# RMSNorm with repeated rows: squares of a tile in one ScalarE instruction, summed by VectorE

## The chip, the core and the metric

The kernel runs on one core of a Trainium2 chip. The core has a vector engine (VectorE, DVE in the profile), a scalar engine (ScalarE, ACT), a GpSimd engine (POOL), a matrix engine that this kernel does not use, and a sync engine (SP). SP and ACT each have a queue from which they start transfers (SPq and ACTq in the profile; the transfers of SP run on queue q1, those of ACT on q10). Sixteen DMA engines move the data between device memory (HBM) and the on-chip memory (SBUF, 128 partitions). The metric is the device time of one execution in microseconds; lower is better.

## The reference

The input `x` has the shape 8 x 512 x 2048 in float32, `gamma` has 2048 elements. Each row of `x` is written out twice in a row, normalized by its root mean square and multiplied by `gamma`:

```
x_rep = np.repeat(x, 2, axis=1)
rms = np.sqrt((x_rep ** 2).mean(axis=-1, keepdims=True) + 1e-6)
out = x_rep / rms * gamma
```

So 33.55 MB come in and 67.11 MB go out, and both copies of a row are the same.

## The kernel before, in words

The 4096 rows are cut into 8 tiles (`ntiles`) of 128 partitions by K = 4 rows. A tile `y` holds R x K = 8 rows per partition, called slots here: `load` (line 45) brings the four input rows into slots 4 to 7, and the result of row k is written to slot 2k and its copy to slot 2k + 1, so that the whole tile is one contiguous run of 64 KB per partition for the store. The writes run ahead of nothing that is still needed: row 0 is in slot 4, which is overwritten only by the result of row 2. The pool `rows` has three such tiles, so the load of tile i + 1 needs the buffer of tile i - 2 and waits for its store to land.

`square` (line 64) squares one row on ScalarE, writes the squares to a scratch tile `sq` in the matrix engine's accumulation memory (PSUM) where nobody reads them, and keeps the row's sum in `ss` by the instruction's accumulator output; it then takes the square root (line 71). `scale` (line 74) takes the reciprocal on VectorE and multiplies the row by it and by `gamma_b` in one instruction (line 77). `repeat` (line 82) copies the result into the neighbouring slot. `compute` (line 85) runs rows one by one: while VectorE scales row k, ScalarE squares row k + 1; the copies of rows 0 to 2 are made by ScalarE, the last one by VectorE.

The order of the work is written out by hand (`manual_schedule`): every engine does its instructions in the order in which the program names them. The loads of tiles 0, 1 and 2 stand at the start, on ACT's queue, the first in four parts. In the loop (line 107), the load of tile i + 1 is issued on ACT's queue ahead of the first square of tile i, from i = 2 on; the load of the last tile has two parts. `store` (line 55) issues on SP's queue once the last copy of its tile is done; the last tile is computed and stored in two halves. The store of tile 5 is cut into runs of 32 KB, all others of whole tiles into runs of 64 KB.

Of the kernel before, what the change touches and what calls it, by code (L numbers as in the profile page):

```python
# [1 line left out]

# [4 lines left out]


@with_exitstack
def kernel(  # L10
    ctx: ExitStack,
    tc: tile.TileContext,
    x: bass.AP,
    gamma: bass.AP,
    out: bass.AP,
):
    nc = tc.nc
    P = nc.NUM_PARTITIONS
    f32 = mybir.dt.float32
    Act = mybir.ActivationFunctionType  # L20
    Alu = mybir.AluOpType

    B, S, D = x.shape
    Bo, So, Do = out.shape
    R = So // S
    assert R == 2 and D == Do and B == Bo and So == S * R
    eps = 1e-6
    inv_d = 1.0 / float(D)


    K = 4
    N = B * S
    assert N % (P * K) == 0
    ntiles = N // (P * K)
    x_t = x.rearrange("b s d -> (b s) d").rearrange("(n p k) d -> n p k d", p=P, k=K)
    out_t = out.rearrange("b s d -> (b s) d").rearrange("(n p j) d -> n p (j d)", p=P, j=K * R)

    singles = ctx.enter_context(tc.tile_pool(name="singles", bufs=1))
    rows = ctx.enter_context(tc.tile_pool(name="rows", bufs=3))
    junk = ctx.enter_context(tc.tile_pool(name="junk", bufs=1, space=bass.MemoryType.PSUM))  # L40
    small = ctx.enter_context(tc.tile_pool(name="small", bufs=8))

    ys = []

    def load(i, eng, parts=1):


        y = rows.tile([P, K * R, D], f32, name="y")
        step = K // parts
        for k in range(0, K, step):  # L50
            at = K * (R - 1) + k
            eng.dma_start(out=y[:, at : at + step, :], in_=x_t[i, :, k : k + step, :])  # L52
        ys.append(y)

    def store(i, k0, k1):

        run = 32768 if i == ntiles - 3 else 65536
        nc.sync.dma_start(  # L58
            out=out_t[i, :, R * k0 * D : R * k1 * D],
            in_=ys[i][:, R * k0 : R * k1, :].rearrange("p j d -> p (j d)"),  # L60
            max_dma_last_dim=run,
        )

    def square(i, k):
        sq = junk.tile([P, D], f32, name="sq")
        ss = small.tile([P, 1], f32, name="ss")
        nc.scalar.activation(  # L67
            out=sq[:], in_=ys[i][:, K * (R - 1) + k, :], func=Act.Square, accum_out=ss[:]
        )
        rms = small.tile([P, 1], f32, name="rms")  # L70
        nc.scalar.activation(out=rms[:], in_=ss[:], func=Act.Sqrt, scale=inv_d, bias=eps_t[:])  # L71
        return rms

    def scale(i, k, rms):
        rstd = small.tile([P, 1], f32, name="rstd")
        nc.vector.reciprocal(out=rstd[:], in_=rms[:])  # L76
        nc.vector.scalar_tensor_tensor(  # L77
            out=ys[i][:, R * k, :], in0=ys[i][:, K * (R - 1) + k, :], scalar=rstd[:], in1=gamma_b[:],
            op0=Alu.mult, op1=Alu.mult,
        )  # L80

    def repeat(i, k, copy):
        copy(out=ys[i][:, R * k + 1, :], in_=ys[i][:, R * k, :])  # L83

    def compute(i, k0, k1):

        rms = square(i, k0)
        for k in range(k0, k1):
            scale(i, k, rms)
            if k + 1 < k1:  # L90
                rms = square(i, k + 1)
                repeat(i, k, nc.scalar.copy)
            else:
                repeat(i, k, nc.vector.tensor_copy)


    ctx.enter_context(tc.manual_schedule())
    load(0, nc.scalar, parts=K)
    gamma_b = singles.tile([P, D], f32, name="gamma_b")
    nc.sync.dma_start(out=gamma_b[0:1, :], in_=gamma.partition_broadcast(1))  # L100
    nc.gpsimd.partition_broadcast(out_ap=gamma_b[:], in_ap=gamma_b[0:1, :])  # L101
    eps_t = singles.tile([P, 1], f32, name="eps_t")
    nc.vector.memset(eps_t, eps)  # L103
    load(1, nc.scalar)
    load(2, nc.scalar)

    for i in range(ntiles):


        if i >= 2 and i + 1 < ntiles:  # L110
            load(i + 1, nc.scalar, parts=2 if i + 2 == ntiles else 1)
        parts = 2 if i == ntiles - 1 else 1
        for k in range(0, K, K // parts):
            compute(i, k, k + K // parts)
            store(i, k, k + K // parts)


# [1 line left out]
_INS = ['x', 'gamma']  # L119
_OUTS = [((8, 1024, 2048), 'float32')]  # L120


# [23 lines left out]
```

## Time and profile before

| | |
|---|---|
| median of 3 runs | 240.74 us (240.67 to 244.2) |
| the profiled execution | 240.8 us, of which the span is 239.0 us |
| moved | 100.69 MB, mean 421 GB/s over the span |
| VectorE busy | 90.8 us (38%), 74 instructions |
| ScalarE busy | 115.8 us (48%), 121 instructions |
| squares (line 67) | 32 of 1872 ns, each with an accumulator read of 186 ns |
| square roots (line 71) | 32 of 294 ns |
| reciprocals (line 76) | 32 of 162 ns |
| scales (line 77) | 32 of 2352 ns |
| copies on ScalarE, on VectorE (line 83) | 23 of 1888 ns, 9 of 1226 ns |

The page gives the busy time of each engine, then the span in 40 slices of 5.98 us with a digit for the busy share in each, then the DMA queues, the chain of work that ended last, and the groups of instructions by line. Times in the timeline are in us from the start of the span. Waits of an engine are listed with what ended them.

### The profile page before, as it was taken

Reading aid. Unit: us, or ns where it says so; the run is one execution under the profiler, and the core shown is the slowest. Engines: PE = TensorE matmul, PEld = TensorE weight load, DVE = VectorE, ACT = ScalarE, POOL = GpSimd, SP = SyncE. Lnnn points to the kernel's source line nnn. Section 1 sums busy time; section 2 is a strip of 40 time slices with the busy share of each in tenths; the row PEclk is TensorE's granted clock in tenths of the full one; section 3 lists DMA queues with packets and bytes.
Section 4 is the critical chain, followed back from the end, with each engine's and each line's share of the span. In section 5 each row is a group of like instructions: output and inputs, shape, how many; then the busy total and the mean of one; then the engine's idle time right before and its main releaser. Section 6 shows DMA issues by size and latency. Waiting matters only on the chain.

```text
span 239.0 us, 295 instructions
## 1 busy us (share of the span) xinstructions
DVE 90.8 (38%) x74; ACT 115.8 (48%) x121; POOL 2.5 (1%) x5
## 2 busy tenths in 40 slices
DVE  0477846006560047600666007460076490072000
ACT  3998992009940089500994019930499550180000
POOL 4000000000000000000000000000000000000000
DMA  7999989989979989999899899799999999898994
GB/s 267 428 447 439 439 351 439 526 351 439 515 345 455 450 374 494 395 411 510 362 428 526 351 439 528 345 444 433 400 430 444 406 499 436 384 505 356 439 428 192
DMA packets 3156, 100.69 MB, mean 421 GB/s; under 512 B 337, under 2 KB 337, under 8 KB 337
## 3 DMA queue, kind: packets, MB, share of 16 engines
q1 hardware_dynamic: 1426, 67.12, 65.0%
q10 hardware_dynamic: 1728, 33.56, 33.3%
q14 instruction: 2, 0.02, 0.0%
HBM read 33.56 MB, written 67.11 MB: 421 GB/s over the span
## 4 chain that ended last, share of the span: by engine, by line
DMA 71%; ACT 10%; DVE 8%; ACTq 1%; issue 0%; SPq 0%
DMA y<-in_x_dram 38%; DMA out_dram<-y 33%; DVE y L77 6%; ACT sq L67 6%; ACT y L83 3%; DVE y L83 2%; ACTq L52 1%; ACT rms L71 1%; DVE rstd L76 0%; SPq L58 0%
## 5 line engine op out<-in xcount | busy, mean ns | idle before, releaser
L67 ACT ACTIVATE sq<-y 128x2048 f32<-128x2048 f32 x32 | 59.9, 1872 | 90.3 <-DMA y<-in_x_dram 74.4
L77 DVE SCALAR_TENSOR_TENSOR y<-y,rstd,gamma_b 128x2048 f32<-128x2048 f32 x32 | 75.3, 2352 | 1.2
L76 DVE RECIPROCAL rstd<-rms 128x1 f32<-128x1 f32 x32 | 5.2, 162 | 123.6 <-ACT rms L71 123.6
L83 ACT COPY y<-y 128x2048 f32<-128x2048 f32 x23 | 43.4, 1888 | 3.6 <-DVE y L77 3.6
L83 DVE COPY y<-y 128x2048 f32<-128x2048 f32 x9 | 11.0, 1226 | 0.3
L71 ACT ACTIVATE rms<-ss,eps_t 128x1 f32<-128x1 f32 x32 | 9.4, 294 | 1.0
L67 ACT ACTIVATION_READ_ACCUMULATOR sq<-y 128x1 f32 x32 | 6.0, 186 | 0.0
L67 ACT ACT_TABLE_LOAD x1 | 1.3, 1283 | 4.1 <-issue 4.1
L101 POOL PARTITION_BROADCAST gamma_b<-gamma_b x1 | 2.3, 2295 | 2.4 <-DMA gamma_b<-in_gamma_dram 2.4
L71 ACT ACT_TABLE_LOAD x1 | 1.3, 1283 | 0.0
L103 DVE MEMSET eps_t<- 128x1 f32 x1 | 0.1, 59 | 0.8 <-PEq L130 0.8
L130 POOL MEMSET const-float32-0.0<- 128x1 f32 x1 | 0.1, 100 | 0.2 <-issue 0.2
L130 POOL MEMSET const-bfloat16-1.0<- 128x1 bf16 x1 | 0.1, 102 | 0.0
L130 POOL MEMSET const-uint8-127<- 128x1 uint8 x1 | 0.1, 102 | 0.0
L130 POOL MEMSET const-float32-1.0<- 128x1 f32 x1 | 0.1, 100 | 0.0
## 6 DMA issues: line engine op xcount, KB each, us to landing
y<-in_x_dram ACTq DMA_DIRECT2D x6, 4096.0 KB, 32.6
out_dram<-y SPq DMA_DIRECT2D x1, 8192.0 KB
out_dram<-y SPq DMA_DIRECT2D x2, 4096.0 KB, 26.4
y<-in_x_dram ACTq DMA_DIRECT2D x4, 1024.0 KB, 7.7
y<-in_x_dram ACTq DMA_DIRECT2D x2, 2048.0 KB, 29.9
out_dram<-y SPq DMA_DIRECT2D x6, 37.5
gamma_b<-in_gamma_dram SPq DMA_DIRECT2D x1, 8.0 KB
```

The costliest lines, as they stand in the source:

```text
L52: eng.dma_start(out=y[:, at : at + step, :], in_=x_t[i, :, k : k + step, :])
L67: nc.scalar.activation(out=sq[:], in_=ys[i][:, K * (R - 1) + k, :], func=Act.Square, accum_out=ss[:])
L71: nc.scalar.activation(out=rms[:], in_=ss[:], func=Act.Sqrt, scale=inv_d, bias=eps_t[:])
L76: nc.vector.reciprocal(out=rstd[:], in_=rms[:])
L77: nc.vector.scalar_tensor_tensor(out=ys[i][:, R * k, :], in0=ys[i][:, K * (R - 1) + k, :], scalar=rstd[:], in1=gamma_b[:], op0=Alu.mult, o ...
L83: copy(out=ys[i][:, R * k + 1, :], in_=ys[i][:, R * k, :])
L101: nc.gpsimd.partition_broadcast(out_ap=gamma_b[:], in_ap=gamma_b[0:1, :])
L103: nc.vector.memset(eps_t, eps)
L130: nc = _bacc.Bacc("TRN2", target_bir_lowering=False, num_devices=1)
```

## The change

Tiles 1 to 6 are computed in another way. One ScalarE instruction squares all four rows (8192 elements per partition) and writes the squares to slots 0 to 3 of the same tile, which hold nothing at that time; VectorE then sums them row by row with one `tensor_reduce` (`total`). Tile 1 does both in halves. One square root and one reciprocal serve the four rows; four scales follow; and the copies are two ScalarE instructions of two rows each. The load of tile i + 1 is issued on ACT's queue after the wide square of tile i, and is one transfer for the last tile too. Tile 0 and the first half of tile 7 keep the square with the accumulator output; in tile 0 the copies of the last two rows are one VectorE instruction. The second half of the last tile puts its squares into slots 1 and 3, which its first half has not filled yet.

At the start, the loads of tiles 0 (now in two parts), 1 and 2 move to SP's queue, and that of `gamma` to ACT's; ScalarE loads the function table that has the square root at once; and the constant `eps_t` is set by GpSimd. The stores all use runs of up to 64 KB. The pool `small` has 4 buffers of four columns.

```diff
-    small = ctx.enter_context(tc.tile_pool(name="small", bufs=8))
+    small = ctx.enter_context(tc.tile_pool(name="small", bufs=4))
...
     def store(i, k0, k1):
-
-        run = 32768 if i == ntiles - 3 else 65536
         nc.sync.dma_start(
             out=out_t[i, :, R * k0 * D : R * k1 * D],
             in_=ys[i][:, R * k0 : R * k1, :].rearrange("p j d -> p (j d)"),
-            max_dma_last_dim=run,
         )
...
+    def slots(i, k0, k1):
+        if i == ntiles - 1 and k0 == H:
+            return slice(1, R * H, R)
+        return slice(k0, k1)
+
+    def square_total(i, k, ss):
         sq = junk.tile([P, D], f32, name="sq")
-        ss = small.tile([P, 1], f32, name="ss")
         nc.scalar.activation(
-            out=sq[:], in_=ys[i][:, K * (R - 1) + k, :], func=Act.Square, accum_out=ss[:]
-        )
...
+            out=sq[:], in_=ys[i][:, K * (R - 1) + k, :], func=Act.Square, accum_out=ss[:, k : k + 1]
         )
...
+    def square(i, k0, k1):
+        nc.scalar.activation(
+            out=ys[i][:, slots(i, k0, k1), :], in_=ys[i][:, K * (R - 1) + k0 : K * (R - 1) + k1, :],
+            func=Act.Square,
+        )
...
+    def total(i, k0, k1, ss):
+        nc.vector.tensor_reduce(
+            out=ss[:, k0:k1], in_=ys[i][:, slots(i, k0, k1), :], op=Alu.add, axis=mybir.AxisListType.X
+        )
+
+    def rsqrt(k0, k1, ss, rstd):
+        nc.scalar.activation(
+            out=rstd[:, k0:k1], in_=ss[:, k0:k1], func=Act.Sqrt, scale=inv_d, bias=eps_t[:]
+        )
+        nc.vector.reciprocal(out=rstd[:, k0:k1], in_=rstd[:, k0:k1])
+
+    def scale(i, k0, k1, rstd):
         for k in range(k0, k1):
...
+            nc.vector.scalar_tensor_tensor(
+                out=ys[i][:, R * k, :], in0=ys[i][:, K * (R - 1) + k, :], scalar=rstd[:, k : k + 1],
+                in1=gamma_b[:], op0=Alu.mult, op1=Alu.mult,
+            )
+
+    def repeat(i, k0, k1, copy=nc.scalar.copy):
+        y_r = ys[i].rearrange("p (k r) d -> p k r d", r=R)
+        copy(out=y_r[:, k0:k1, 1, :], in_=y_r[:, k0:k1, 0, :])
...
-    load(0, nc.scalar, parts=K)
+    load(0, nc.sync, parts=2)
     gamma_b = singles.tile([P, D], f32, name="gamma_b")
-    nc.sync.dma_start(out=gamma_b[0:1, :], in_=gamma.partition_broadcast(1))
+    nc.scalar.dma_start(out=gamma_b[0:1, :], in_=gamma.partition_broadcast(1))
+    nc.scalar.preload_act_table(Act.Sqrt)
+    eps_t = singles.tile([P, 1], f32, name="eps_t")
+    nc.gpsimd.memset(eps_t, eps)
     nc.gpsimd.partition_broadcast(out_ap=gamma_b[:], in_ap=gamma_b[0:1, :])
-    eps_t = singles.tile([P, 1], f32, name="eps_t")
-    nc.vector.memset(eps_t, eps)
-    load(1, nc.scalar)
-    load(2, nc.scalar)
+    load(1, nc.sync)
+    load(2, nc.sync)
 
     for i in range(ntiles):
+        ss = small.tile([P, K], f32, name="ss")
+        rstd = small.tile([P, K], f32, name="rstd")
+        if i == 0:
+            for k0 in (0, H):
+                for k in range(k0, k0 + H):
+                    square_total(i, k, ss)
+                rsqrt(k0, k0 + H, ss, rstd)
+                scale(i, k0, k0 + H, rstd)
+            repeat(i, 0, H)
+            repeat(i, H, K, nc.vector.tensor_copy)
+        elif i < ntiles - 1:
+            for k0, k1 in ((0, H), (H, K)) if i == 1 else ((0, K),):
+                square(i, k0, k1)
+                total(i, k0, k1, ss)
...
-        if i >= 2 and i + 1 < ntiles:
-            load(i + 1, nc.scalar, parts=2 if i + 2 == ntiles else 1)
-        parts = 2 if i == ntiles - 1 else 1
-        for k in range(0, K, K // parts):
-            compute(i, k, k + K // parts)
-            store(i, k, k + K // parts)
+            if i >= 2:
+                load(i + 1, nc.scalar)
+            rsqrt(0, K, ss, rstd)
+            scale(i, 0, K, rstd)
+            repeat(i, 0, H)
+            repeat(i, H, K)
+        else:
+            for k in range(H):
+                square_total(i, k, ss)
+            rsqrt(0, H, ss, rstd)
+            square(i, H, K)
+            scale(i, 0, H, rstd)
+            total(i, H, K, ss)
+            rsqrt(H, K, ss, rstd)
+            repeat(i, 0, H)
+            store(i, 0, H)
+            scale(i, H, K, rstd)
+            repeat(i, H, K)
+        store(i, H if i == ntiles - 1 else 0, K)
```

Here H = K // 2 = 2.

## The prediction

> **What bounds the kernel now.** First the page's slices and the DMA queues. The DMA engines are busy in every slice but the first and the last, while VectorE and ScalarE work in bursts with pauses.
>
> ```profile
> DVE 90.8 (38%) x74; ACT 115.8 (48%) x121; POOL 2.5 (1%) x5
> DMA  7999989989979989999899899799999999898994
> DMA packets 3156, 100.69 MB, mean 421 GB/s; under 512 B 337, under 2 KB 337, under 8 KB 337
> ```
>
> Second, two stretches cut from one landing of a store to the next, with the columns stretch, length, busy time of DVE, ACT and POOL, PE clock, DMA share, GB/s:
>
> ```profile
> 80.60:109.60 29.00, 11.20 (x9) 14.36 (x15) 0.00 (x0) 1.00 1.00 434
> 109.65:138.64 28.99, 11.20 (x9) 14.36 (x15) 0.00 (x0) 1.00 1.00 434
> ```
>
> One tile (4.19 MB in, 8.39 MB out) takes W = 29.0 us of full DMA; at 434 GB/s a store alone is 19.3 us and a load 9.7. Third, the timeline of one tile (start, length, engine, line):
>
> ```profile
> 109.65 0.34 ACTq L52 DMA_DIRECT2D y<-in_x_dram  x1
> 113.31 1.88 ACT L67 ACTIVATE sq<-y 128x2048 f32<-128x2048 f32 x1 [14.14 <-DMA y<-in_x_dram]
> 129.02 1.23 DVE L83 COPY y<-y 128x2048 f32<-128x2048 f32 x1
> 130.33 0.33 SPq L58 DMA_DIRECT2D out_dram<-y  x1
> 138.64 0.33 ACTq L52 DMA_DIRECT2D y<-in_x_dram  x1
> ```
>
> From the first square to the store's issue it is 130.33 - 113.31 = 17.0 us: call this C. The load at 138.64 waits for a store to land, so the new store was queued 138.64 - 130.33 = 8.3 us before the ring was empty. That is the only slack. Compute is hidden as long as C grows by less than about 8 us. Fourth, who gets the DMA when a load and a store are both queued: in the window 85 to 108,
>
> ```profile
> q1 hardware_dynamic: 96, 6.29, 63.1%
> q10 hardware_dynamic: 111, 3.64, 36.6%
> ```
>
> (q1 is SP's queue, the stores; q10 ACT's, the loads). A load gets a little over a third: its rows are 32 KB long, the store's 64 KB. So a load issued beside a store is slow: 109.65 to about 142.3, 32.7 us, though alone it would take 9.7.
>
> **What the Trainium skill says.** "VectorE: DVE Perf Modes", The perf-mode tier table: tensor_reduce runs at 1x only, whatever the type. No reduce is in this trace; the 1x operation in it (L77, 2352 ns for 2048) is (2048 + 210)/0.96, as that rate wants. "ScalarE: Activation LUTs", What ACT_TABLE_LOAD costs: an ACTIVATE with immediate scale and bias takes 186 ns + 0.833 ns per element; for 2048 that is 1892, the trace has 1872 (L67) and 1888 (copy, L83), so it agrees. "DMA: Bandwidth & Descriptors", Queues, rings and completion order: an engine round-robins between the queues packet by packet; with 64 against 32 KB that is 2 to 1, and the 63 to 37 above agrees.
>
> **The new chain of one tile (tiles 2 to 6).** Wide square 8192 x 0.833 + 186 = 7.01 us (page's price; 4 x 1.87 = 7.5 from the row is the upper end). Reduce of 8192, which can't start earlier: (8192 + 151)/0.96 = 8.69 us, an estimate by the fit that the same VectorE page gives in its errata section for fp32 tensor_tensor; 8.75 by the 210 of L77. Sqrt 0.29, reciprocal 0.16. Four scales, back to back 2.38 each with the handoff (215.44 - 213.06 in the chain): 9.50. The last wide copy, 4096 x 0.833 + 186 = 3.60; the first lies beside scales 3 and 4. Six handoffs of 0.02 to 0.03: 0.15. Sum C' = **29.4 us**, 12.4 more than now. What was interleaved by row (square beside scale) is now serial. ACT is in order, so square(i+1) starts only after the last copy of tile i: C' is also the least period, against W = 29.0.
>
> Engine totals don't matter: ACT some 14.5 us and DVE 18.4 per tile.
>
> **The moved load.** load(i+1) now stands behind the wide square on ACT, 7.1 us after its start, no longer in front. It has store(i-2) to wait for, long landed by then; what is queued behind it (sqrt, copies) is idle anyway during the reduce. But until then the newest store has the DMA alone, and then has two thirds of it. The load ends last: with the store 7.1 us ahead, 12.2 us of it remain, over in 18.4; the load has had 6.1 of its 9.7 by then and 3.5 more alone. So it ends W after the store's first byte. Now add the latencies: issue to first byte 0.8 us and last byte to landing 1.8 us, estimates from the start (issue at 0.72, DMA share 0.56 already between 1 and 2 us; gamma lands at 2.79) and from the tail (last store lands 21.3 us after 216.77, at 238.1, when bytes had ended by about 236.3). If no load overlaps, square(i+1) comes 31.6 us after store(i-1)'s issue, and store(i) 29.4 after square(i): two tiles take 61.0 us where DMA alone would take 58.0.
>
> **The walk** (us). Start: loads 0 to 2 move from ACT's to SP's queue, gamma the other way. Tile 0 in two halves of 4.8 us each: the first lands at 0.72 + 2.1 (gamma's 0.72 to 2.79) + 4.8 = 7.6, the second at 12.5; two squares with their accumulator reads 4.1, to 16.6; sqrt and reciprocal 0.5, two scales 4.8, to 21.9; the DVE copy of both rows 2.3 to 2.5 (2 x 1.23): store 0 at 24.4, now 23.8. Covered: the DMA has load 2 until about 32, and store 0 is now behind it on the same ring. Were that cover gone it would cost 0.6. The table load saved (1.28), eps on POOL (0.1, before gamma lands) and four DMA issues of 0.3 to 0.9 on SP ahead of its first store lie in the same cover: nothing. Store 0 lands at 52.9 as now, bytes ended 51.1. Tile 1: square at 22.6, in halves 2 x 3.6, reduces of 4.42 end at 35.0, then 0.5, scales 45.1, copy: store 1 at 48.7, in time.
>
> - square 2 at 48.7, load 3 issued 55.8; store 1 + load 3 end 80.1, landing 81.9 = square 3. Store 2 at 78.1, in time.
> - store 2 + load 4 end 109.1. Store 3 at 81.9 + 29.4 = 111.3 = square 4, first byte 112.1: **DMA idle 3.0**.
> - store 3 + load 5 end 141.1, landing 142.9 = square 5. Store 4 at 140.7, first byte 141.5: idle 0.4.
> - store 4 + load 6 end 170.5. Store 5 at 172.3 = square 6, first byte 173.1: **idle 2.6**.
> - store 5 + load 7 end 202.1, landing 203.9 = square 7. Store 6 at 201.7: idle 0.4; its bytes end 221.9.
> - Last tile: squares, sqrt, scales and reduce 13.8, sqrt and reciprocal, first copy: half store at 203.9 + 17.8 = 221.7: idle 0.6. The second half follows at 226.6, behind 9.7 us of the first: in time.
>
> Idle in all 7.0 us, all on the path since the DMA has no slack. The removed 32 KB rows of the third-last store and the unsplit last load change no bytes; I take nothing, and from -1 to +1 us (one round of packets each way). The small pool's 4 buffers bring no wait: each is reused four tiles later.
>
> The profiled execution took 240.8 us with a span of 239.0; the median is 240.74, the same. **240.8 + 7.0 = 247.8, say 248**, 3% slower.
>
> **Bounds of the unknowns.** Latencies together between 2.1 (gamma) and 3.3: -1 to +2. Reduce and square together 1 us cheaper: less idle at two places, -2 or nothing, because a store issued sooner pushes its 64 KB rows (2.4 us) between the last rows of the load. Square at its upper end: +0.5 at three chains in a row, +1.5. This gives 245 to 252.
>
> **Rivals.**
> - *The cover holds* (ends on the other side, not slower). If a load got half of the DMA beside a store, it would land 19.4 + 2.6 = 22.0 us after issue, just inside the 22.3 that the chain still has; then stores come every 29.4 and the first backlog hides the 0.4: 241, at most 243. It decides from a share of one half up. The 63 to 37 and the landings of 32.7 us speak against it; that the split is by packet count (96 to 111) in a coarse window leaves it open. 0.15.
> - *The new forms cost more*: a reduce or a square into the tile's own slots that runs at, say, 3 us more per tile. C' of 32.4 then sets every period: about 6 x 3 less what overlaps, 253 to 260. L83's copy to the same memory at 1888 speaks against. 0.12.
> - *The DMA gets faster* from fewer mixed stretches: 434 GB/s is held in both mixed and pure stretches, so only the 1 to 2 us of dips could go; under 236 would need 2% more rate. 0.03.
>
> Forecast 0.68; 0.02 for a start that fails to hide. The range takes the forecast's 245 to 252, and reaches to 243 and to 254 into the two nearest rivals. Two per cent, 4.8 us, is about what a measurement of this kernel can tell from no change: slower by over 2% (above 245.6) is most of the forecast, the second rival and a little of the rest, 0.75; faster 0.03; within 0.22.
>
> **What would show it.** Square at 7.0 us, reduce 8.7, copy 3.6; square to store issue 29.4 in tiles 2 to 6; loads landing 24 to 26 us after issue; DMA share below 0.9 around 109 to 112 and 170 to 173, at 1.0 before 100; stores landing 30 to 31 us apart; ACT's waits for the load alternate between about 0 and 2 to 4 us. It is wrong if the load lands under 22 us from its issue (first rival), or if the DMA stays at 434 GB/s to the end.

## The result, and the profile after

The changed kernel takes 251.59 us (median of 4 executions, 249.72 to 253.26) against 240.70: 1.045 times the kernel before, 95% interval 1.034 to 1.055. The profiled execution took 253.26 us with a span of 251.5. Here and below a ratio leaves out executions more than 1.5% above the fastest of the same kernel, and a median keeps them.

The same lines of the page as before (busy time; DMA share in 40 slices, now of 6.29 us; packets), and the groups of the new operations:

```profile
DVE 134.5 (53%) x51; ACT 115.6 (46%) x46; POOL 2.6 (1%) x6
DMA  7999998979989899968999988999979937989995
DMA packets 2595, 100.68 MB, mean 400 GB/s; under 512 B 289, under 2 KB 289, under 8 KB 289
L83 DVE TENSOR_REDUCE ss<-y 128x4 f32<-128x8192 f32 (+1 forms) x8 | 56.6, 7084 | 69.9 <-ACT y L77 69.9
L77 ACT ACTIVATE y<-y 128x8192 f32<-128x8192 f32 (+1 forms) x8 | 45.9, 5743 | 16.6 <-DMA y<-in_x_dram 16.6
L102 ACT COPY y<-y 128x4096 f32<-128x4096 f32 x15 | 54.1, 3603 | 37.3 <-DVE y L95 37.3
```

The bytes are the same, but the DMA is no longer busy in every slice. VectorE is busy for 43.7 us more, but still for no more than 53% of the span. What matters is the order. From the timeline (start, length, engine, line) around tile 3:

```profile
48.33 7.02 ACT L77 ACTIVATE y<-y 128x8192 f32<-128x8192 f32 x1
52.77 0.36 ACTq L53 DMA_DIRECT2D y<-in_x_dram  x1
...
77.57 0.33 SPq L57 DMA_DIRECT2D out_dram<-y  x1
85.04 7.03 ACT L77 ACTIVATE y<-y 128x8192 f32<-128x8192 f32 x1 [7.49 <-DMA y<-in_x_dram]
85.05 0.33 ACTq L53 DMA_DIRECT2D y<-in_x_dram  x1
...
111.87 0.33 ACTq L53 DMA_DIRECT2D y<-in_x_dram  x1
114.17 7.02 ACT L77 ACTIVATE y<-y 128x8192 f32<-128x8192 f32 x1
114.29 0.33 SPq L57 DMA_DIRECT2D out_dram<-y  x1
```

(52.77, 85.05 and 111.87 are the issues of loads 3, 4 and 5; 77.57 and 114.29 those of stores 2 and 3.) Load 3 takes 32.3 us, from 52.77 to 85.02. ScalarE waited for it for 7.5 us, and the store of tile 2 was queued beside it from 77.57 on. From square to store issue it is 114.29 - 85.04 = 29.25 us. The DMA meanwhile finished what it had. Two of its stops, cut out as stretches (length, busy DVE, ACT and POOL, clock, DMA share, GB/s):

```profile
109.00:112.00 3.00, 1.63 (x1) 2.01 (x2) 0.00 (x0) 1.00 0.15 66
```

```profile
203.00:206.00 3.00, 2.58 (x2) 2.01 (x2) 0.00 (x0) 1.00 0.18 76
206.00:208.00 2.00, 0.00 (x0) 2.00 (x1) 0.00 (x0) 1.00 0.00 0
208.00:210.00 2.00, 0.00 (x0) 2.00 (x2) 0.00 (x0) 1.00 0.00 0
```

That is 3.00 x (1 - 0.15) = 2.6 us and, in the three lines together, 6.5 us without transfers. Between them the rate is lower as well. The same stretch before and after, in that order:

```profile
118.00:198.00 80.00, 37.46 (x31) 44.97 (x46) 0.00 (x0) 1.00 1.00 432
```

```profile
118.00:198.00 80.00, 46.70 (x15) 32.47 (x10) 0.00 (x0) 1.00 0.99 417
```

80 x (1 - 417/432) = 2.8 us. The span is 12.5 us longer; 2.6 + 6.5 + 2.8 = 11.9 of them are these.

The second long wait, for load 6, has a part of its own. The trace has sixteen landings for each transfer, one for each DMA engine's share, and the square that uses it starts only after the last of them. Of load 6 (issued at 145.64) fifteen shares are there by 175.22, the last at 180.00. Of the loads' queue (q10) only one row starts in the window 175.3 to 178.8:

```profile
q1 hardware_dynamic: 17, 1.05, 69.1%
q10 hardware_dynamic: 1, 0.03, 2.2%
```

```profile
180.02 7.03 ACT L77 ACTIVATE y<-y 128x8192 f32<-128x8192 f32 x1 [7.50 <-DMA y<-in_x_dram]
```

So 4.8 of these 7.5 us are the lag of one engine.

### The profile page after: what moved, and what is told of

Read it like the earlier page. It is cut to its first block, busy times and chain, and to the rows that moved or that the text cites. A ratio compares the mean times of both kernels' runs of the same rounds, so it can differ in the third digit from the quotient of the medians.

```text
span 251.5 us, 193 instructions
## 1 busy us (share of the span) xinstructions
DVE 134.5 (53%) x51; ACT 115.6 (46%) x46; POOL 2.6 (1%) x6
## 4 chain that ended last, share of the span: by engine, by line
DMA 35%; DVE 34%; ACT 21%; issue 1%; SPq 0%
DMA y<-in_x_dram 35%; DVE y L95 18%; DVE ss L83 16%; ACT y L77 12%; ACT y L102 6%; ACT sq L71 2%; ACT rstd L88 1%; DVE rstd L91 0%; SPq L53 0%
## 5 line engine op out<-in xcount | busy, mean ns | idle before, releaser
L83 DVE TENSOR_REDUCE ss<-y 128x4 f32<-128x8192 f32 (+1 forms) x8 | 56.6, 7084 | 69.9 <-ACT y L77 69.9
L95 DVE SCALAR_TENSOR_TENSOR y<-y,rstd,gamma_b 128x2048 f32<-128x2048 f32 x32 | 74.0, 2349 | 0.7
L102 ACT COPY y<-y 128x4096 f32<-128x4096 f32 x15 | 54.1, 3603 | 37.3 <-DVE y L95 37.3
L77 ACT ACTIVATE y<-y 128x8192 f32<-128x8192 f32 (+1 forms) x8 | 45.9, 5743 | 16.6 <-DMA y<-in_x_dram 16.6
L88 ACT ACTIVATE rstd<-ss,eps_t 128x4 f32<-128x4 f32 (+1 forms) x10 | 3.0, 296 | 54.9 <-DVE ss L83 54.8
L71 ACT ACTIVATE sq<-y 128x2048 f32<-128x2048 f32 x6 | 11.3, 1880 | 5.9 <-DMA y<-in_x_dram 5.8
L91 DVE RECIPROCAL rstd<-rstd 128x4 f32<-128x4 f32 (+1 forms) x10 | 1.7, 173 | 22.9 <-ACT rstd L88 22.9
L102 DVE COPY y<-y 128x4096 f32<-128x4096 f32 x1 | 2.3, 2295 | 0.0
L71 ACT ACTIVATION_READ_ACCUMULATOR sq<-y 128x1 f32 x6 | 1.1, 186 | 0.0
```

The lines of the kernel that those rows point to most:

```text
L71: nc.scalar.activation(out=sq[:], in_=ys[i][:, K * (R - 1) + k, :], func=Act.Square, accum_out=ss[:, k : k + 1])
L77: nc.scalar.activation(out=ys[i][:, slots(i, k0, k1), :], in_=ys[i][:, K * (R - 1) + k0 : K * (R - 1) + k1, :], func=Act.Square,)
L83: nc.vector.tensor_reduce(out=ss[:, k0:k1], in_=ys[i][:, slots(i, k0, k1), :], op=Alu.add, axis=mybir.AxisListType.X)
L88: nc.scalar.activation(out=rstd[:, k0:k1], in_=ss[:, k0:k1], func=Act.Sqrt, scale=inv_d, bias=eps_t[:])
L91: nc.vector.reciprocal(out=rstd[:, k0:k1], in_=rstd[:, k0:k1])
L95: nc.vector.scalar_tensor_tensor(out=ys[i][:, R * k, :], in0=ys[i][:, K * (R - 1) + k, :], scalar=rstd[:, k : k + 1], in1=gamma_b[:], op0= ...
```

## The experiments

All ratios are to the kernel before, run on the same chip beside them, with the 95% interval in brackets; the times are medians. Experiments 1 to 4, 5 to 8 and 9 to 12 ran on three chips, on which the medians of the kernel before differ by no more than 0.1 us (240.67 to 240.76).

**1. Half of the sum.** The changed kernel, with a shorter reduce:

```diff
-            out=ss[:, k0:k1], in_=ys[i][:, slots(i, k0, k1), :], op=Alu.add, axis=mybir.AxisListType.X
+            out=ss[:, k0:k1], in_=ys[i][:, slots(i, k0, k1), 0 : D // 2], op=Alu.add, axis=mybir.AxisListType.X
```

> The changed kernel, but the VectorE sum reads only the first half of each row's squares, so half of the sum is left out; everything else is as in the changed kernel. The chain from square to store issue is 4.3 us shorter in tiles 2 to 6, about 25 us. Theory (the longer chain uses up the 8.3 us that the store was queued early): 17.0 + 8.3 = 25.3, so this one should just fit again, 241 to 244 us. Rival (the new start, the queue of the loads, the store runs or the tail cost the time): 249 to 253 as the changed kernel.

Measured: ratio 1.031 (1.026 to 1.035), 248.4 us. The reduce is 4.3 us shorter, and the chain, 25.0 us (87.16 to the store at 112.15), fits within the theory's 25.3; yet only 3 us come back, so the theory fails. Load 3 was issued at 52.73, as in the changed kernel, and landed 34.4 us later, just ahead of its square at 87.16. Fifteen engines had landed their shares by 84.13, the last one at 87.14.

**2. Equal rows.** The changed kernel, all stores in 32 KB runs:

```diff
             in_=ys[i][:, R * k0 : R * k1, :].rearrange("p j d -> p (j d)"),
+            max_dma_last_dim=32768,
         )
```

> The changed kernel with every store cut into runs of 32 KB, so that a load gets one of two rows rather than one of two and a half of the bytes. Theory (the load's third of the DMA makes it land 32 us after its issue, later than the 29.4 us chain needs it): loads land 20 to 25 us after issue, no square waits for its load, period 29.4, 241 to 243 us. Rival (the 29.4 us chain alone sets the time, the share does not matter): 249 to 253.

Measured: ratio 1.001 (0.998 to 1.004), 240.35 us. The whole loss is gone, with the 29.4 us chain, the new start, the late place of the load and the new tail all in place. Who gets the DMA in the window 60 to 77 of the changed kernel (q1 stores, q10 loads; the shares of packets that straddle the edges make the sum exceed 100%), and in 85 to 105 of this one:

```profile
q1 hardware_dynamic: 80, 5.24, 71.1%
q10 hardware_dynamic: 78, 2.56, 34.8%
```

```profile
q1 hardware_dynamic: 128, 4.19, 48.6%
q10 hardware_dynamic: 128, 4.19, 48.6%
```

In both a load's row alternates with a store's row (80 packets to 78, 128 to 128); only the length of the store's row differs. Load 4 of this kernel, from its timeline:

```profile
81.73 0.33 ACTq L53 DMA_DIRECT2D y<-in_x_dram  x1
...
107.02 7.03 ACT L78 ACTIVATE y<-y 128x8192 f32<-128x8192 f32 x1 [0.18 <-DMA y<-in_x_dram]
```

25.3 us, a little longer than expected, but just when the chain is free: the wait is 0.18 us. The last engine's share of a load comes at most 0.9 us after the one before it. The stretch 118 to 198 is back at 432 GB/s:

```profile
118.00:198.00 80.00, 50.36 (x18) 39.26 (x14) 0.00 (x0) 1.00 1.00 432
```

So the length of the stores' rows is the cause. It acts through the load's share of the DMA, and also through how late the landing is seen and how far engines fall behind (last section); this run changes all three and doesn't price them apart.

**3. The load ahead of the square.** The changed kernel:

```diff
         elif i < ntiles - 1:
+            if i >= 2:
+                load(i + 1, nc.scalar)
             for k0, k1 in ((0, H), (H, K)) if i == 1 else ((0, K),):
...
-            if i >= 2:
-                load(i + 1, nc.scalar)
             rsqrt(0, K, ss, rstd)
```

> The changed kernel with the load of tile i + 1 issued ahead of the wide square of tile i, as in the kernel before. Theory: the load's place is worth little, since in the trace the ACT queue issued it at the start of the wide square, not at its end; where it had to wait for the square's own load, it was some 5 us later than the store's landing allowed, and the DMA had a store to do meanwhile: 247 to 252 us. Rival (the late load is the cause): 241 to 244.

Measured: ratio 1.031 (1.027 to 1.034), 248.1 us. As expected: 3.5 us come back, most of the loss stays.

**4. Sums by the accumulator output.** The changed kernel:

```diff
-            for k0, k1 in ((0, H), (H, K)) if i == 1 else ((0, K),):
-                square(i, k0, k1)
-                total(i, k0, k1, ss)
-
             if i >= 2:
                 load(i + 1, nc.scalar)
+            for k in range(K):
+                square_total(i, k, ss)
             rsqrt(0, K, ss, rstd)
```

> The changed kernel, but tiles 1 to 6 square row by row with the accumulator output instead of one wide square and a VectorE sum; the load of tile i + 1 stands ahead of the squares. One square root and reciprocal per tile, wide copies, start, queues, runs and tail as in the changed kernel. The chain is 4 x 2.06 + 0.5 + 9.5 + 3.6 = 22 us. Theory: under 25 us, so hidden, 239 to 242 us. Rival (the rest of the change costs the time): 249 to 253.

Measured: ratio 1.032 (1.029 to 1.035), 248.5 us. The theory fails here plainly: without the VectorE sum and with a chain of 22 us the kernel is no better than with 25. Load 3 lands 34.4 us after its issue (52.86 to 87.30), load 5 even 37.1. So a chain of 29 us is not needed for a loss; late loads are enough. That gave a new theory: a load's row waits for a store's row as long as stores are queued, and what counts is how late the loads land, the last one above all. It points at the one store that had 32 KB runs, that of tile 5, beside which the last load runs.

**5. The run taken from the kernel before.**

```diff
-        run = 32768 if i == ntiles - 3 else 65536
+        run = 65536
```

> The kernel before with the store of tile 5 in runs of 64 KB like the others, nothing else. First theory (the longer chain): 240 to 241.5, the runs of one store are worth nothing. New theory (a 32 KB row of a load waits for a 64 KB row of a store as long as stores are queued, so the last load lands late and the last tile's stores come after the DMA has run dry): the second half of the last load lands 5 to 10 us later and 3 to 6 us of DMA idle appear after 215 us: 243 to 247 us.

Measured: ratio 1.012 (1.002 to 1.022), 243.9 us. In the timeline of this kernel the second half of the last load lands at 219.70, where it was 208.06; that is 11.6 us later, more than the 5 to 10 expected:

```profile
219.70 1.88 ACT L67 ACTIVATE sq<-y 128x2048 f32<-128x2048 f32 x1 [17.20 <-DMA y<-in_x_dram]
```

and by then the stores have run out (stretches as above):

```profile
224.00:226.00 2.00, 1.97 (x3) 1.60 (x2) 0.00 (x0) 1.00 0.72 311
226.00:228.00 2.00, 1.97 (x2) 0.54 (x1) 0.00 (x0) 1.00 0.15 66
228.00:230.00 2.00, 0.33 (x1) 0.00 (x0) 0.00 (x0) 1.00 0.61 262
```

One argument of one store is worth 3.2 us by the medians; by the interval of the ratio, from 0.6 to 5.3 us.

**6. The run given back to the changed kernel.**

```diff
+        run = 32768 if i == ntiles - 3 else 65536
         nc.sync.dma_start(
...
+            max_dma_last_dim=run,
```

> The changed kernel with the 32 KB runs given back to the store of tile 5 alone. First theory: no change, 249 to 253. New theory in its strong form (the removed run is all of it): 240 to 242. In its weak form (the long chain with 64 KB rows loses DMA time at about 110 and 205 us, the run only helps the last load): 245 to 249.

Measured: ratio 1.031 (1.022 to 1.040), 249.1 us. The strong form fails. By the medians 2.5 of the 10.9 us come back, but 249.1 lies on the border between the weak form and no change, and the interval overlaps that of the changed kernel: between these two the run doesn't decide. In the traces the last load is not faster for it, 26.6 us from issue to landing (174.05 to 200.61) against 26.5 in the changed kernel (180.03 to 206.51).

**7. Both: row sums and the run.** Experiment 4 with the edit of 6.

> The changed kernel with row-by-row accumulating squares in tiles 1 to 6 (chain about 22 us), the load ahead of them, and 32 KB runs for the store of tile 5. If the removed run explains the 248.5 us of the same kernel without it: 240 to 243. If the unsplit last load and the rewritten last tile explain it: 245 to 249.

Measured: ratio 1.017 (1.008 to 1.026), 245.4 us; 3.1 us less than without the run, and at the lower end of the second expectation. So the removed run explains some 3 us here, and 4.7 us are left.

**8. The chain alone.** The kernel before, with tiles 2 to 6 computed as in the changed kernel and nothing else of it:

```diff
+    def serial(i):
+        ss = small.tile([P, K], f32, name="ss4")
+        rstd = small.tile([P, K], f32, name="rstd4")
+        nc.scalar.activation(out=ys[i][:, 0:K, :], in_=ys[i][:, K : 2 * K, :], func=Act.Square)
+        nc.vector.tensor_reduce(out=ss[:], in_=ys[i][:, 0:K, :], op=Alu.add, axis=mybir.AxisListType.X)
...
+        if 2 <= i < ntiles - 1:
+            serial(i)
+            store(i, 0, K)
+            continue
```

> The kernel before, but tiles 2 to 6 are computed as in the changed kernel (one wide square into the tile's own slots, VectorE sum, one square root, four scales, two wide copies); loads, queues, start, store runs and last tile stay as before. Chain 29.4 us instead of 17.0. If the chain alone costs the time: 246 to 251. If it takes the runs of the tile 5 store or the unsplit last load as well: 240 to 244.

Measured: ratio 1.030 (1.022 to 1.038), 248.5 us: 7.8 us for the chain alone, with 64 KB rows beside it. The stores are issued at 82.54, 111.67, 143.15, 173.97 and 204.05, on the mean 30.4 us apart. Tile 3 to 4, from its timeline:

```profile
82.42 7.02 ACT L100 ACTIVATE y<-y 128x8192 f32<-128x8192 f32 x1
82.54 29.46 SPq L58 DMA_DIRECT2D out_dram<-y  x2
...
113.52 0.33 ACTq L52 DMA_DIRECT2D y<-in_x_dram  x1
113.90 7.03 ACT L100 ACTIVATE y<-y 128x8192 f32<-128x8192 f32 x1 [2.26 <-DMA out_dram<-y]
```

The store of 82.54 lands at 113.5 and only then is the next load, load 5, issued, with the square behind it. That square's own data, load 4, had landed at 106.24: this wait of 2.26 us comes from the place of the load ahead of the square. The next two squares wait 1.59 and 0.86 us for their loads.

**9. The split of the last load.** Experiment 7 with

```diff
-                load(i + 1, nc.scalar)
+                load(i + 1, nc.scalar, parts=2 if i + 2 == ntiles else 1)
```

> The row-sum kernel with 32 KB runs for the store of tile 5 (245.4 us), and now with the load of the last tile in two halves as in the kernel before. What is left of it against the kernel before is 4.7 us. If the unsplit last load is the rest: 240 to 242.5. If it is the chain of 22 us with its wide copies, or the new start: 244.5 to 246.5.

Measured: ratio 1.027 (1.019 to 1.034), 247.4 us. Not faster, and above both expectations, so the unsplit last load is not the rest of experiment 7. What is stays open.

**10. Equal rows, longer chain.** Experiment 2 with a second, superfluous sum:

```diff
     def total(i, k0, k1, ss):
+        nc.vector.tensor_reduce(
+            out=ss[:, k0:k1], in_=ys[i][:, slots(i, k0, k1), 0 : D // 2], op=Alu.add, axis=mybir.AxisListType.X
+        )
         nc.vector.tensor_reduce(
```

> The changed kernel with all stores in 32 KB runs (240.4 us), and the VectorE sum of each tile preceded by a sum over the first half of each row, whose result is written over: chain 33.5 us. Theory (with equal rows the period is the larger of the DMA's 29.0 and the chain): stores 33.5 us apart, 262 to 268 us. Rival (equal rows hide any chain, the chain was never a limit): 240 to 246.

Measured: ratio 1.100 (1.098 to 1.102), 264.6 us, and stores 33.6 us apart (53.21, 86.80, 120.39 and on). With equal rows and this chain no square of tiles 2 to 6 waits for its load, and the chain alone is the period.

**11. The start alone.** The kernel before with the new start:

```diff
-    load(0, nc.scalar, parts=K)
+    load(0, nc.sync, parts=2)
...
-    nc.sync.dma_start(out=gamma_b[0:1, :], in_=gamma.partition_broadcast(1))
+    nc.scalar.dma_start(out=gamma_b[0:1, :], in_=gamma.partition_broadcast(1))
+    nc.scalar.preload_act_table(Act.Sqrt)
...
-    load(1, nc.scalar)
-    load(2, nc.scalar)
+    load(1, nc.sync)
+    load(2, nc.sync)
```

> The kernel before with the start of the changed kernel alone (loads 0 to 2 on SP's queue, the first in two parts, gamma on ACT's queue, table load, constant on GpSimd). Theory: covered by load 2, 239.5 to 241.5. Rival (the store of tile 0 now lies behind load 2 on the same queue, which moves the rows of later loads against the stores): 242 to 245.

Measured: ratio 1.004 (1.001 to 1.007), but the median of 21 executions is 243.5: nine of them lie at 240.4 to 241.1 and nine above 244, up to 248.1, where of the kernel before 3 of 24 do. The profile at hand is of one of the longer ones (246.9). What makes it long stands at its end, where the DMA share is about that of one engine in sixteen (0.06) for 7 us; the others are done:

```profile
236.00:243.00 7.00, 0.00 (x0) 0.00 (x0) 0.00 (x0) 1.00 0.07 28
```

Fifteen shares of the last store are there by 236.4, the last at 244.0. A single late engine shows early, too: load 3, issued at 52.69, lands at 87.36, 34.7 us later, while fifteen shares were there by 84.1:

```profile
87.36 1.88 ACT L67 ACTIVATE sq<-y 128x2048 f32<-128x2048 f32 x1 [19.38 <-DMA y<-in_x_dram]
```

Whether the start makes such executions more frequent is left open: the medians and the counts speak for it, and the ratio, formed as said with the result, can't speak on it. Why an engine falls behind is not shown.

**12. Equal rows for the kernel before.**

```diff
-        run = 32768 if i == ntiles - 3 else 65536
+        run = 32768
```

> The kernel before with all stores in 32 KB runs. Theory: its 17.0 us chain has slack with either rows, so the earlier landing of loads buys nothing: 239.5 to 241. Loads land 20 to 27 us after issue instead of 32. Rival (half-size rows cost DMA rate): 242 to 246; or (late loads still cost the kernel before something): under 239.

Measured: ratio 1.007 (1.004 to 1.009), 242.1 us, over the expected 241 and in the range of the first rival. But that rival's reason is not in the trace: from 118 to 198 the rate is 433 GB/s, against 432. Here too engines end unevenly: of the last store the first engine's share is there at 236.0 (236.1 in the kernel before), the last at 239.2 against 238.1. A kernel whose chain has slack gains nothing from early loads, and this one pays 0.7%.

No version of these beats both kernels: experiment 2 equals the kernel before.

## Why the prediction was right, by its own steps

The direction, the range (243 to 254) and the mechanism hold: the serial chain outgrows its cover, because loads that get a third of the DMA land late, and the DMA runs dry between tiles. Experiment 8 has the long chain without the rest of the change: 7.8 us, where the sum said 7.0, with the stores 30.4 us apart where two tiles in 61.0 were predicted, though one of its three waits ends with a store and not with a load. Experiments 2 and 10 take the two conditions apart. With half of the DMA for a load the loss is gone, though the chain is the same; with half of the DMA and a chain of 33.5 the chain is the period. The total of 248 was 3.6 us low, and that it came so near is in part luck, as the terms show: the idle times were of other sizes or ended otherwise than in the walk, and two of the five loads (3 and 6) took 32.3 and 34.4 us, where the prediction named 24 to 26 as a sign.

- **The chain, 29.4 us.** Right: square 7.02, reduce 8.69, scales 9.27 together (9.50 was taken), copy 3.60; 29.25 in the trace. The estimates from the Trainium skill were met to 0.01 us: (8192 + 151)/0.96 is 8.69, by the fit that "VectorE: DVE Perf Modes" gives for fp32 tensor_tensor in its section on the TRN2 errata, and the reduce here follows it; 8192 x 0.833 + 186 is 7.01, from "ScalarE: Activation LUTs", What ACT_TABLE_LOAD costs.
- **The load "stands behind the wide square on ACT, 7.1 us after its start".** Wrong. It was issued at 52.77 in the middle of a square, at 85.05, 0.01 us after one had started, and at 111.87 even 2.3 us before the square ahead of it started. This transfer, which needs nothing from the square, doesn't wait for its end. What it waits behind is the square's own wait for its load: load 4 was held until load 3 had landed.
- **"Landing 81.9 = square 3."** Too early by 3.1 us. The walk let load 3 end alone. But store 2 was queued at 77.57 and put rows of 64 KB ahead of the load's last rows. The bounds had named this; the walk should have had it. The 1.8 us from last byte to landing was also a misreading: it came from a tail in which the engines ended unevenly. From the last row's end to the landing it is 2.8 us here (last section).
- **Idle of 3.0 at 109 to 112 and 2.6 at 170 to 173.** The first was there, 2.6, but it ended otherwise. In the walk it ends with the first byte of store 3, and load 5 follows 7.1 us after the square. In the trace load 5 comes first: it is issued at 111.87, store 3 at 114.29. That the size fits is luck. The second came at 203.6 to 210, with 6.5: instead of alternating, every third tile waited 7.5 us for its load (stores at 77.57, 114.29, 143.42, 172.55, 209.28: gaps of 36.7, 29.1, 29.1, 36.7), the second time mostly for one engine. The 2.8 us of lower rate in between were not in the sum at all. Together it is 11.9 us in the profiled execution, against 7.0 in the sum; that execution lies 5.3 us above 248, the median 3.6. Two of the four executions are 3.4 us shorter (249.72 and 249.93 against twice 253.26), and what they lack is not known, as the trace is of a longer one.
- **The third-last store's runs: "I take nothing, and from -1 to +1 us".** Wrong for the kernel before: 3.2 us by the medians. Their bytes are the same, but there they decide when the last load lands. For the changed kernel experiment 6 doesn't settle it.
- **The start, "covered: nothing".** Not settled by experiment 11.
- **"The only slack" of 8.3 us.** Not a constant that a new chain may use up: with chains of 25.0 and 22 us in the changed kernel (experiments 1 and 4) 248.4 and 248.5 us remain. In the five traces that have the new start and store 2 issued before 75 us (experiments 1, 4, 7, 9, 11) load 3 lands 34.4 to 34.9 us after issue, in the kernel before and experiment 5 31.4. These 3 us are the lag of one to three engines: in all five traces the other thirteen to fifteen have landed their shares by 84.1, some 31.4 us after issue. Why these lag was not tried. The effects don't add up either: the chain alone (7.8) and the run alone (3.2) happen to make 11.0, but giving back any one of run (2.5), place (3.5) or half the reduce (3.2) returns about 3 us each, by the medians.
- **The rivals.** The first had the right condition: at a share of one half the cover does hold (experiment 2), with loads landing at 25.3 instead of 22.0 us and still in time. The second and third did not come: each form ran at its price, and the DMA did not get faster (417 GB/s from 118 to 198 us, against 432).

## What to carry to other kernels

When load and store share the DMA, look at the length of their rows, not only at the rate: the DMA alternated by rows here, so a load with rows of half the length got a third, and its landing, not the bandwidth, became the limit of the next tile. Before making a tile's work serial, compare the chain from load landing to store issue with the DMA's time for a tile, and add what a load really takes beside a store. Look at the landing of each engine's share, too: the slowest one releases the next tile. If a chain must be long, equal rows can give it the cover back; and where one transfer of many has a different run, find out which transfer beside it that serves.

## What the runs showed of the hardware

- Two queues share the DMA row by row: 5.24 to 2.56 MB with rows of 64 and 32 KB, 4.19 to 4.19 with 32 and 32, at 432 GB/s in total both in the kernel before and in experiment 2 (118 to 198). "DMA: Bandwidth & Descriptors", Queues, rings and completion order, says that an engine turns to the next queue at packet boundaries; the packets that the trace counts here are the whole rows.
- ScalarE's queue issues a transfer while the ACTIVATE ahead of it is still running: at 52.77, with the square running from 48.33 to 55.35. At 111.87 it issues one 2.3 us before the ACTIVATE ahead of it starts, while copies still run.
- A load's landing waits for a row of the store as well. From the end of a load's last row to its landing it is 0.3 to 0.4 us in the changed kernel where no store's row is queued beside it (loads 4 and 7), 2.8 us beside rows of 64 KB (loads 3, 5 and 6), and 1.6 us in experiment 2 beside rows of 32 KB. The differences, 2.4 and 1.2 us, are the times of one row of 64 and of 32 KB on an engine in these traces (2.42 and 1.21 us).
- The sixteen engines do not keep in step. One of them landed its share of load 6 of the changed kernel 4.8 us after the other fifteen, and its share of the last store in the profile of experiment 11 7.6 us after them, and no run shows why; with all rows of 32 KB (experiment 2) it is at most 0.9 us for a load.
